# A fourth pair of rounded weight parts in the mixer of a hybrid decoder block, and the first slots of the expert ring moved to other memory

## The chip, the cores and the metric

The kernel runs on one core of a Trainium2 chip. The metric is the device time of one execution in microseconds (us), the median of several runs. The engines are called by the names of the profile: PE (TensorE matmul), PEld (its weight loads), DVE (VectorE), ACT (ScalarE), POOL (GpSimd) and SP (SyncE, whose queue SPq issues nearly all transfers).

## The reference, cut to what matters

One decoder block on 256 tokens of width 1024, all in fp32. A mixer comes first: one projection of x onto 5376 columns (`w_in`) feeds an RWKV-7 recurrence (8 heads of 64), a causal attention (8 heads of 64) and two sigmoid gates; the two branches go through their own weights, are gated, added and projected by `w_out`. Then a layer norm, a router that takes 4 of 32 experts for each token, and the experts:

```
proj   = x @ w_in                                  # 256 x 5376
merged = gate0 * (rwkv7(proj) @ w_branch_rwkv) + gate1 * (attention(proj) @ w_branch_attn)
x      = layer_norm(alpha * x + merged @ w_out)
h      = x[tokens of e] @ expert_w_in[e] + b       # 1024 x 2048, fp32, for each of 32 experts
y      = swiglu(h) @ expert_w_out[e] + b           # 1024 x 1024
out    = layer_norm(alpha * x + sum over 4 experts of weight * y)
```

The expert weights are 32 x 12 MB of fp32 and dominate the traffic.

## The kernel before, in words

**The mixer's products.** `w_in` is taken in 21 jobs of 256 columns, each in two halves of 512 KB (`load_col`, into one of RAWS = 4 buffers `wr`). A half is split into two rounded parts, a high one `wh` (a cast on ACT, line 208) and a low one `wl` (raw minus high, line 209, on POOL for the first half of a job and on DVE for the second; on DVE for both in the first two jobs). The products run on PE as three fp32r passes (high x high, high x low, low x high, `three`, line 322), 24 matmuls for a half, all recorded at line 131. The pool of parts has PARTS = 3 buffers of each kind: a half can be split only when the products of the half three before it are done. In the rows that follow, a half's buffers carry numbers, so wl_853 is the low part of one particular half.

**What the products are mixed with.** A planner written out at line 825 interleaves four generators on PE: the two halves of the recurrence (`rwkv_half`, four heads each), the attention, and the 21 jobs (`gemms`), in an order that its own estimates (WAIT, `spent`) decide while the program is built. Within each half of the recurrence stands a solve (lines 539 to 558): eight masked copies out of PSUM (L528), four scatters (L539), a transposition (L544), a loop of 15 small pairs of instructions on DVE (L551, L552), a product with a mask (L553), a transposition back (L555), and four copies on ACT (L558). PE then transposes that result (`w<-ident,ring` in the first half, `w<-ident,kr` in the second, line 564) and goes on with many small matmuls.

**Memory.** The expert weights go through a ring of 10 slots (`stream`, line 788). Slots are taken in the order 0 to 9; seven of them hold 2 MB, and slot 8 holds 3 MB. Until the mixer is over, five 2 MB blocks at the left of the memory (`slot_e(0)` to `slot_e(4)`) hold its long-lived data, two tensors each: x_t and low_t (x, and the inputs of the low-rank parts), h0a and h0b, h0c and half_t, inv_t and y_t8, and the gates. Each becomes a slot when its data are no longer wanted: block 0 is slot 0, block 1 slot 1, block 2 slot 2, blocks 3 and 4 slots 5 and 6. In `next_job` (line 368) three loads of 2 units (1 MB each) are issued between the loads of `w_in` once the low-rank parts, the first half of the recurrence and the second solve are done.

**After the mixer.** `branch_weights(n)` (line 921) loads the branch weights of four column groups, n = 0 to 3, and asks for ring loads up to 8, 8, 10 and 10 units (line 933). `out_weights(k)` (line 984), k = 0 to 7, loads 512 KB of `w_out` each, splits it into parts, and asks for up to 10, 10, 10, 12, 12, 12, 12 and 14 units. On DVE, the low part of `out_weights(0)` stands ahead of `merge(2)`, which gates and adds the third column group, and of a copy of the layer-norm vectors (`gbc`, line 967) that PE waits for before it begins the products with `w_out`. All transfers of these places go through SP's one queue, in the order in which they are issued. Then come the layer norm, the routing and 32 experts, eight 1 MB units of `expert_w_in` and four of `expert_w_out` each; a slot is loaded again when PE has used it.

Of the kernel before, what the change touches and what calls it, by code (L numbers as in the profile page):

```python
# [9 lines left out]
F32 = mybir.dt.float32  # L10
F32R = mybir.dt.float32r
# [7 lines left out]
P = 128  # L19
# [17 lines left out]
WAIT = {"d1": 36.12, "d2": 25.0, "d3": 36.78, "lo": 5.97, "kk": 4.39, "rk": 2.07, "bt": 6.5, "bk": 2.55, "unit": 0.5,  # L37
        "sub": 18, "xm": 1.3, "mg": 1.02, "mg2": 1.0, "ws": 0.71, "us": 0.49, "y": 0.73, "gn": 2.77, "rope": 2.21,
        "sm": 3.6, "tr": 0.81, "s1": 13.02}
# [11 lines left out]
PARTS = 3  # L51
UNIT = 2048
# [66 lines left out]
def hybrid_block_kernel(ctx: ExitStack, tc: tile.TileContext, A, out):  # L119
# [21 lines left out]
    def slot_e(i):  # L141
        return ring.tile([P, 2 * UNIT], F32, name="ring%d" % i)

    x_t, low_t, h0a, h0b, h0c, half_t, inv_t, y_t8, *gates = (t[:, i * UNIT:(i + 1) * UNIT] for t in map(slot_e, range(5)) for i in range(2))
    gates = [t.rearrange("p (q j t) -> p q j t", q=2, j=4) for t in gates]
    ident = const.tile([P, P], F32, name="ident")
    iota = const.tile([P, CAP], F32, name="iota")
# [10 lines left out]
    def half(name):  # L158
        return (raws_ if name == "wr" else parts).tile([P, 1024], F32, name=name)

    mx = ExitStack()
    tmp_ctx = ExitStack()
    px_ctx = ExitStack()
    pg = px_ctx.enter_context(tc.tile_pool(name="pg", bufs=2, space=PSUM))
    pw = px_ctx.enter_context(tc.tile_pool(name="pw", bufs=4, space=PSUM))
    pa = px_ctx.enter_context(tc.tile_pool(name="pa", bufs=2, space=PSUM))
    sp = tmp_ctx.enter_context(tc.tile_pool(name="sp", bufs=1, side="right"))
    ap_ = tmp_ctx.enter_context(tc.tile_pool(name="ap", bufs=1, side="right"))
    cp = tmp_ctx.enter_context(tc.tile_pool(name="cp", bufs=1, side="right"))
# [25 lines left out]
    x_t = x_t.rearrange("p (k t) -> p k t", k=KD)  # L195
# [5 lines left out]

    def split(raw, n, engine):

        hi, lo = half("wh").bitcast(F32R), half("wl").bitcast(F32R)
        s = 1024 // n
        for i in range(n):
            sl = slice(i * s, (i + 1) * s)
            nc.scalar.copy(out=hi[:, sl], in_=raw[:, sl])  # L208
            engine.tensor_tensor(out=lo[:, sl], in0=raw[:, sl], in1=hi[:, sl].bitcast(F32), op=ALU.subtract)  # L209
        return [t.rearrange("p (k c) -> p k c", k=4) for t in (hi, lo)]  # L210
# [68 lines left out]
        nc.scalar.copy(out=xh[:, sl, :], in_=x_t[:, sl, :])  # L279
        nc.vector.tensor_tensor(out=xl[:, sl, :], in0=x_t[:, sl, :], in1=xh[:, sl, :].bitcast(F32), op=ALU.subtract)  # L280

    lora_parts = [[half(n).bitcast(F32R) for n in ("wh", "wl")] for _ in range(2)]

    def split_lora(n, i):
        i, j = divmod(n * i, 4)
# [8 lines left out]
    lora_parts = [[t.rearrange("p (k c) -> p k c", k=4) for t in w] for w in lora_parts]  # L294
# [58 lines left out]
    def next_job():  # L353
        if asked:
            asked.sort(key=lambda a: a[0][0] == "a")
            key, col, use, raws, gemm = asked.pop(0)
        elif "v0" in done and len(free_gates) > (8 - EARLY_GATES if "rwkv0" not in done else LATE_GATES if min(at(n) for n in range(3)) < 1e9 else 0):
            g = free_gates.pop(0)
            key, col, use, raws, gemm = "gate%d" % g, GATE0 + g * 256, lambda ps: gate(g, ps), None, gemm_cm
        else:  # L360
            return None
        if key == "lora":
            return key, use, gemm, [lambda w=w: w for w in lora_parts]
        early_ = raws is not None
        raws = raws or load_col(col)
        if key == "v0":
            constants()
        for after, wait, n in (("low", WAIT["d1"], 2), ("rwkv0", WAIT["d2"], 4), ("sub1", WAIT["d3"], 6)):
            if done.get(after, 1e9) + wait <= spent[0] and len(tiles) < n:
                stream(n)  # L370
        engines = [nc.vector] * 2 if early_ else [nc.gpsimd, nc.vector]
        return key, use, gemm, [lambda i=i: split(raws[i], 2 if early_ else 1, engines[i]) for i in range(2)]
# [409 lines left out]
    while sum(takes) < len(views):  # L782
        n = sum(takes)
        takes.append(min(sizes[len(takes)] if len(takes) < len(slots) else 2 - n % 2, len(views) - n))
    tiles, pieces = [], []
    later = {n: lambda i=i: slot_e(i) for i, n in enumerate((0, 1, 2, 5, 6))}

    def stream(n):

        while len(tiles) < n:  # L790
            n_ = len(pieces) % len(slots)
            if slots[n_] is None:
                slots[n_] = later[n_]()
            slot = slots[n_]
            u0, m = len(tiles), takes[len(pieces)]
            pieces.append(u0)
            i = 0
            while i < m:
                src, k = views[u0 + i]
                j = i + 1  # L800
                if k is None:
                    dst = slot[:, i * UNIT:j * UNIT].rearrange("p (q k c) -> p q k c", q=len(src), k=KD // 2)
                    for q, v in enumerate(src):
                        fetch(out=dst[:, q], in_=v)
                else:
                    while j < m and views[u0 + j][0] is src and views[u0 + j][1] == k + j - i:
                        j += 1
                    fetch(out=slot[:, i * UNIT:j * UNIT], in_=src[:, k * UNIT:(k + j - i) * UNIT])
                i = j
            tiles.extend(slot[:, i * UNIT:(i + 1) * UNIT] for i in range(m))  # L810
# [10 lines left out]
    def at(n):  # L821
        r = ready[n]
        return done.get(r[0], 1e9) + r[1] if isinstance(r, tuple) else r
# [4 lines left out]
    while min(at(n) for n in range(3)) < 1e9 or "gate7" not in done:  # L828
        n = min((n for n in range(4) if at(n) <= spent[0]), default=None)
# [3 lines left out]
        if n < 3 and since >= FILL and at(3) <= spent[0]:  # L833
            n = 3
        wait = next(tasks[n], 1e9)
        since = 0 if n == 3 else since + 1
        if wait is None and min(at(i) for i in range(3)) <= spent[0]:
            wait = 0.0
        if wait is None:

            spent[0] = max(spent[0], min(at(n) for n in range(3)))
            wait = 0.0
        ready[n] = wait if isinstance(wait, tuple) else spent[0] + wait
    stream(6)
    nc.gpsimd.tensor_copy(out=tri, in_=cm[:, M_SC:M_SC + P])
    mx.close()
    tmp_ctx.close()
# [6 lines left out]
    def slot_of(i):  # L854
        return slot_pools[i].tile([P, sizes[i] * UNIT], F32, name="ring")

    later.update((i, lambda i=i: slot_of(i)) for i in (3, 4, 7, 8, 9))
    for i in (9, 3, 4):
        slot_pool(i, side="right")
    slot_b = slot_of(9)  # L860
    slot_b = [slot_b[:, i * UNIT:(i + 1) * UNIT] for i in range(2)]
# [59 lines left out]
    def branch_weights(n):  # L921

        ns = slice(n * 256, (n + 1) * 256)
        raws = load(wba[:, :, ns], wbr[:, :, ns])
        if n == 2:
            fetch(out=gbr, in_=A["norms"])
            fetch(out=bo, in_=L("expert_b_out"))
            fetch(out=rw, in_=A["router_by_rows"].rearrange("(k p) e -> p k e", p=P))
            fetch(out=rb, in_=L("router_b").partition_broadcast(P))
        if n == 0:  # L930
            for b in range(NB):
                fetch(out=x1[:, b, :], in_=A["x_by_rows"][b * P:(b + 1) * P, :])
        stream((8, 8, 10, 10)[n])
        w = []
        for i, raw in enumerate(raws):
            hi, lo = half("wh").bitcast(F32R), half("wl").bitcast(F32R)
            halved(hi, lo, raw, 1, [("pool", "dve")[(i + 1) % 2]] * 2)
            w.append([t.rearrange("p (k c) -> p k c", k=4) for t in (hi, lo)])
        branch.append(w)
# [525 lines left out]
    for kind, e in steps:  # L1465
        i = e % 2
# [147 lines left out]
```

## Time and profile before

| | us |
|---|---|
| median of 3 runs | 1241.23 |
| lowest and highest run | 1229.15, 1243.23 |
| the profiled execution's own time | 1234.5 |
| its span, first to last instruction | 1232.3 |
| mean granted clock of PE | 0.983 of 2.4 GHz |

The profile is of one execution, whose own time is 2.2 us more than its span. Times in the trace are from the span's start. The matmuls' ends are modelled and overlap the next one, so that the distance between two starts tells more than a duration.

### The profile page before, as it was taken

The numbers are of one execution on the slowest core, as the hardware profiler recorded it, in microseconds if no ns is written. First come the engines' busy times: TensorE is split into PE (matmuls) and PEld (weight loads), VectorE is DVE, ScalarE is ACT, GpSimd is POOL, SyncE is SP. The second block draws the span as 40 slices with busy tenths as digits, with TensorE's granted clock in tenths as the row PEclk, the third lists the DMA queues.
The fourth block names the chain that finished last, engine by engine and source line by source line (L and its number), as shares of the span: only waits on it lengthen the run. The fifth ranks groups of instructions, "written<-read, shape, count | busy, mean of one in ns | idle before, by whom it ended". The sixth has DMA issues, their size and how long they took to land. (4 is left out here: it accounts for less than half of the span.)

```text
span 1232.3 us, 15098 instructions
## 1 busy us (share of the span) xinstructions
PE 1145.2 (93%) x6396; PEld 580.3 (47%) x6396; DVE 404.1 (33%) x767; ACT 263.9 (21%) x486; POOL 94.2 (8%) x69
## 2 busy tenths in 40 slices
PE   9989989999999999999989887989898998989996
PEld 7778778897434343443424223423232333333423
DVE  5975783385502313130202111211112121212123
ACT  7456443554111010111101000101010101010211
POOL 3322121152300000000000000000000000000001
PEclk9989997999999999999999998999999999999999
DMA  8434244497999999999999999999999999999994
GB/s 269 121 102 155 81 160 167 147 340 266 414 429 428 426 427 429 426 427 428 427 428 427 425 430 395 390 425 429 428 426 427 428 427 428 428 427 426 429 424 162
DMA packets 62272, 439.80 MB, mean 357 GB/s; under 512 B 5662, under 2 KB 34168, under 8 KB 37528
## 3 DMA queue, kind: packets, MB, share of 16 engines
q1 hardware_dynamic: 61624, 437.67, 86.6%
q8 instruction: 52, 0.85, 0.3%
q0 software_dynamic: 144, 0.79, 0.2%
q10 hardware_dynamic: 432, 0.33, 0.1%
q14 instruction: 20, 0.16, 0.0%
HBM read 437.71 MB, written 1.05 MB: 356 GB/s over the span
## 5 line engine op out<-in xcount | busy, mean ns | idle before, releaser
L131 PE MATMUL h<-ring,xg 128*64 128x512 f32 x2048 | 459.6, 596 | 26.6 <-DMA ring<-in_expert_w_in_dram 25.4
L131 PEld LDWEIGHTS h<-ring,xg 128*64 128x64 f32 x2048 | 143.5, 136 | 308.2 <-issue 287.3
L131 PE MATMUL y<-ring,at 128*64 128x512 f32 x992 | 222.8, 596 | 27.5 <-DMA ring<-in_expert_w_out_dram 26.0
L1314 DVE TENSOR_SCALAR h<-h 128x512 f32<-128x512 f32 x32 | 22.4, 700 | 395.4 <-PE h L131 395.4
L131 PEld LDWEIGHTS y<-ring,at 128*64 128x64 f32 x992 | 68.9, 137 | 168.8 <-issue 134.4
L1315 ACT ACTIVATE lc<-h 128x512 f32<-128x512 f32 x32 | 19.1, 597 | 514.0 <-DVE h L1314 499.5
L131 PE MATMUL g<-xh,wh 128*128 128x256 f32 x304 | 95.6, 314 | 2.9 <-ACT rope_s L707 2.1
L1349 DVE TENSOR_TENSOR acc<-acc,t 128x512 f32<-128x512 f32 x56 | 38.5, 687 | 173.7 <-PE t L131 173.7
L131 PE MATMUL g<-xh,wl 128*128 128x256 f32 x304 | 87.9, 289 | 1.4 <-DVE wl L209 1.4
L131 PE MATMUL g<-xl,wh 128*128 128x256 f32 x304 | 87.5, 288 | 0.0
L1338 ACT COPY yp<-y 64x512 f32<-64x512 f32 x62 | 35.9, 579 | 212.3 <-PE y L131 211.7
L131 POOL TENSOR_TENSOR acc<-acc,x 128x256 f32<-128x256 f32 x4 | 3.9, 993 | 903.2 <-DVE ln_rs L131 903.0
L131 PEld LDWEIGHTS g<-xh,wh 128*128 128x128 f32 x304 | 59.4, 195 | 12.6 <-issue 8.1
L1115 PE MATMUL t<-oh,x 128*128 128x128 f32 x480 | 59.5, 284 | 5.9 <-DVE oh L1101 5.9
L1115 PEld LDWEIGHTS t<-oh,x 128*128 128x128 f32 x480 | 56.6, 197 | 17.7 <-issue 17.3
L131 PEld LDWEIGHTS g<-xl,wh 128*128 128x128 f32 x304 | 59.6, 196 | 2.2 <-issue 2.2
L131 PEld LDWEIGHTS g<-xh,wl 128*128 128x128 f32 x304 | 59.6, 196 | 1.9 <-DVE wl L209 1.6
L131 PE MATMUL t<-yp,ct 128*128 128x512 f32 (+1 forms) x124 | 56.5, 598 | 0.7 <-ACT yp L1338 0.7
L209 POOL TENSOR_TENSOR wl<-wr,wh 128x1024 fp32r<-128x1024 f32 x18 | 43.2, 2402 | 138.3 <-ACT wh L208 128.9
L208 ACT CAST wh<-wr 128x1024 fp32r<-128x1024 f32 (+1 forms) x44 | 42.1, 969 | 44.6 <-PE g L131 32.7
L131 PEld LDWEIGHTS t<-yp,ct 128*128 128x128 f32 x124 | 22.3, 189 | 34.6 <-issue 32.3
L1118 ACT ACTIVATE xg<-t,gbc 128x128 f32<-128x128 f32 x60 | 27.4, 457 | 42.5 <-PE t L1115 24.9
(373 smaller groups left out, 1070.0 us busy)
## 6 DMA issues: line engine op xcount, KB each, us to landing
ring<-in_expert_w_in_dram SPq DMA_DIRECT2D x127, 2048.0 KB, 39.1
ring<-in_expert_w_out_dram SPq DMA_DIRECT2D x61, 2048.0 KB, 39.1
wr<-in_w_in_dram SPq DMA_DIRECT2D x40, 512.0 KB, 4.0
wr<-in_w_out_by_rows_dram SPq DMA_DIRECT2D x8, 512.0 KB, 5.1
ring<-in_expert_w_out_dram SPq DMA_DIRECT2D x4, 1024.0 KB, 26.1
wr<-in_w_branch_attn_dram SPq DMA_DIRECT2D x4, 512.0 KB, 7.3
wr<-in_w_branch_rwkv_dram SPq DMA_DIRECT2D x4, 512.0 KB, 8.8
ring<-in_expert_w_in_dram SPq DMA_DIRECT2D x2, 1024.0 KB, 16.1
```

The costliest lines, as they stand in the source:

```text
L131: queues[e] = make(*a, **k)
L208: nc.scalar.copy(out=hi[:, sl], in_=raw[:, sl])
L209: engine.tensor_tensor(out=lo[:, sl], in0=raw[:, sl], in1=hi[:, sl].bitcast(F32), op=ALU.subtract)
L1115: last = nc.tensor.matmul(ps[:, i * ns:(i + 1) * ns], lhsT=x1[:, b, k * P:(k + 1) * P], rhs=oh[:, b, :], start=b == 0 and i == 0, stop=b = ...
L1118: def scaled(ps, n, k0, put=lambda e, make, **a: make(**a)):
L1314: nc.vector.tensor_scalar(out=gate_, in0=gate_, scalar1=7.0, scalar2=None, op0=ALU.min)
L1315: nc.scalar.activation(out=lc4, in_=g4, func=AF.Sigmoid, scale=1.702)
L1338: nc.scalar.copy(out=yp[r0_:r0_ + CAP, dh * 512:(dh + 1) * 512], in_=y[dh * CAP:(dh + 1) * CAP, :])
L1349: nc.vector.tensor_tensor(out=acc[:, b, hs], in0=acc[:, b, hs], in1=ps, op=ALU.add)
```

## The change

x_t and low_t leave block 0 of the ring and get a pool of their own (`ep`) at the right end of the memory, with the pools that are given back when the mixer is over. Once x has been split, the memory of x_t is used as a fourth pair of parts: `pair_of` gives every fourth half the two halves of that tile in place of `wh` and `wl`. The blocks of the ring are four instead of five: h0a and h0b are slot 0, h0c and half_t slot 1, the last two blocks slots 5 and 6 as before. Slots 2, 3 and 4 lie in the memory given back with the mixer, slot 4 in that of `ep`. The load after the low-rank parts is dropped, and the targets of `stream` after the mixer are 2 units lower until n = 3.

```
-    x_t, low_t, h0a, h0b, h0c, half_t, inv_t, y_t8, *gates = (... map(slot_e, range(5)) for i in range(2))
+    h0a, h0b, h0c, half_t, inv_t, y_t8, *gates = (... map(slot_e, range(1, 5)) for i in range(2))
+    given = [0]
+    def pair_of():
+        given[0] += 1
+        if given[0] % (PARTS + 1) or not more:
+            return half("wh").bitcast(F32R), half("wl").bitcast(F32R)
+        t = more[0].tile([P, UNIT], F32, name="xt").bitcast(F32R)
+        return t[:, 0:1024], t[:, 1024:2048]
+    ep = tmp_ctx.enter_context(tc.tile_pool(name="ep", bufs=1, side="right"))
+    more = [ep]
+    x_t, low_t = (ep.tile([P, UNIT], F32, name=n) for n in ("xt", "low"))
     def split(raw, n, engine):
-        hi, lo = half("wh").bitcast(F32R), half("wl").bitcast(F32R)
+        hi, lo = pair_of()
-        for after, wait, n in (("low", WAIT["d1"], 2), ("rwkv0", WAIT["d2"], 4), ("sub1", WAIT["d3"], 6)):
+        for after, wait, n in (("rwkv0", WAIT["d2"], 2), ("sub1", WAIT["d3"], 4)):
-    later = {n: lambda i=i: slot_e(i) for i, n in enumerate((0, 1, 2, 5, 6))}
+    later = {n: lambda i=i: slot_e(i) for i, n in ((1, 0), (2, 1), (3, 5), (4, 6))}
-    stream(6)
+    stream(4)
+    more.clear()
-    later.update((i, lambda i=i: slot_of(i)) for i in (3, 4, 7, 8, 9))
-    for i in (9, 3, 4):
+    later.update((i, lambda i=i: slot_of(i)) for i in (2, 3, 4, 7, 8, 9))
+    for i in (4, 9, 2, 3):
         slot_pool(i, side="right")
-        stream((8, 8, 10, 10)[n])
+        stream((6, 6, 8, 10)[n])
```

PE's instructions stand in the same order as before from the first to the last. On ACT, DVE and POOL the splits move forward against the rest. On DVE, the first solve before (the small pairs are L551 and L552, the splits L209; the rows are taken from its start, its middle and its end):

```order
L209 TENSOR_TENSOR wl_783<-wr_776,wh_782 128x1024
L551 TENSOR_TENSOR ring3_64<-ring3_64 128x15
...
L715 TENSOR_TENSOR ak_810<-ak_810,rope_t_811 128x512
L552 TENSOR_TENSOR ring3_64<-ring3_64 128x6x10
L209 TENSOR_TENSOR wl_853<-wr_846,wh_852 128x1024
L551 TENSOR_TENSOR ring3_64<-ring3_64 128x5x11
...
L553 TENSOR_TENSOR ring2_63<-ring3_64,cf_107 128x512
L555 STREAM_TRANSPOSE ring3_64<-ring2_63 128x512
L209 TENSOR_TENSOR wl_948<-wr_941,wh_947 128x1024
```

Here wl_783 stands ahead of the loop's first pair, wl_853 ahead of the pair that is 55 wide on its way down, and wl_948 behind the transposition L555. The same place in the changed kernel, whose lines are 13 higher (the fourth pair is xt, here xt_783 and xt_947, and the small pairs are L564 and L565):

```order
L222 TENSOR_TENSOR xt_783<-wr_777,xt_783 128x1024
L552 TENSOR_TENSOR ring3_63<-sc_t_151,cf_111 32x16x16 x4
...
L564 TENSOR_TENSOR ring3_63<-ring3_63 128x11x5
L222 TENSOR_TENSOR wl_853<-wr_846,wh_852 128x1024
L565 TENSOR_TENSOR ring3_63<-ring3_63 128x11x5
...
L566 TENSOR_TENSOR ring2_62<-ring3_63,cf_111 128x512
L222 TENSOR_TENSOR xt_947<-wr_941,xt_947 128x1024
L568 STREAM_TRANSPOSE ring3_63<-ring2_62 128x512
```

The half 783 is split ahead of the four scatters instead of behind them, the half 853 six steps of the loop sooner, and the half 947 ahead of the transposition back instead of behind it. On SP, the loads of the first ring slots between those of `w_in`, as a difference:

```order
-L131 DMA wr<-in_w_in_dram 128x4x256 x18
-L131 DMA ring_1493<-in_expert_w_in_dram 128x4096
+L131 DMA wr<-in_w_in_dram 128x4x256 x26
+L131 DMA ring_1858<-in_expert_w_in_dram 128x4096
 L131 DMA wr<-in_w_in_dram 128x4x256 x8
-L131 DMA ring_1864<-in_expert_w_in_dram 128x4096
-L131 DMA wr<-in_w_in_dram 128x4x256 x8
-L131 DMA ring_2457<-in_expert_w_in_dram 128x4096
+L131 DMA ring_2449<-in_expert_w_in_dram 128x4096
```

The first of the three ring loads is gone; the other two stand where they stood. Further on SP, behind the branch weights of n = 3, also as a difference:

```order
 L131 DMA wr<-in_w_branch_attn_dram 128x4x256
 L131 DMA wr<-in_w_branch_rwkv_dram 128x4x256
+L131 DMA ring<-in_expert_w_in_dram 128x4096
 L131 DMA wr<-in_w_out_by_rows_dram 128x1024 x4
-L131 DMA ring_2907<-in_expert_w_in_dram 128x4096
+L131 DMA ring_2905<-in_expert_w_in_dram 128x4096
```

There a 2 MB load is new, between the last branch weights and the first weights of `w_out`; from the load after those four on, both kernels have asked for equally many units.

## Rows read from the trace of the kernel before

**Rows 1.** The page's second part: what the transfers moved, in GB/s, in 40 equal slices of the span, 30.8 us each.

```profile
GB/s 269 121 102 155 81 160 167 147 340 266 414 429 428 426 427 429 426 427 428 427 428 427 425 430 395 390 425 429 428 426 427 428 427 428 428 427 426 429 424 162
```

**Rows 2.** The page's sixth part, transfers by their issue: out<-in, queue, operation, count, size of one, median us from issue to landing.

```profile
ring<-in_expert_w_in_dram SPq DMA_DIRECT2D x127, 2048.0 KB, 39.1
```

**Rows 3.** The timeline of SP at the end of the mixer and behind it: start of the issue, us, queue, line, operation, count (the us of a row with a count reach from the first issue to the last).

```profile
247.91 0.50 SPq L131 DMA_DIRECT2D ring<-in_expert_w_in_dram  x1
...
251.03 0.38 SPq L131 DMA_DIRECT2D wr<-in_w_branch_rwkv_dram  x1
255.03 8.83 SPq L131 DMA_DIRECT2D wr<-in_w_out_by_rows_dram  x4
...
294.01 1.28 SPq L131 DMA_DIRECT2D ring<-in_expert_w_out_dram  x3
```

**Rows 4.** What PE waited for in the first 250 us: engine, tile and line that waited, engine, tile and line that released it; us in total, times, longest us.

```profile
PE g L131 <- DVE wl L209: 8.3, 3, 3.4
PE g L131 <- ACT rope_s L707: 2.1, 1, 2.1
```

**Rows 5.** The timeline of PE: start, us, engine, line, operation, and in brackets how long the engine sat idle before it and for whom. The rows at 96.82 and 104.62 are the first and last of one and the same run of products in the first half of the recurrence as 193.68 and 206.82 are in the second.

```profile
21.01 2.59 PE L131 MATMUL w<-ring 64*128 64x256 f32 x12
...
76.85 0.39 PE L131 MATMUL g<-wl,xh 128*128 128x256 f32 x1 [3.44 <-DVE wl L209]
...
77.63 4.22 PE L131 MATMUL w<-ring 64*128 64x256 f32 x12
...
86.69 1.04 PE L131 MATMUL w<-ident,ring 128*128 128x128 f32 x8
...
96.82 0.55 PE L131 MATMUL a<-ident,sm 128*128 128x128 f32 x3
...
104.62 0.27 PE L131 MATMUL w<-ring,sc_t 64*64 64x64 f32 x1
...
167.76 0.39 PE L131 MATMUL g<-xh,wl 128*128 128x256 f32 x1 [1.42 <-DVE wl L209]
...
177.06 0.55 PE L131 MATMUL g<-wl,xh 128*128 128x256 f32 x1 [3.43 <-DVE wl L209]
...
183.56 1.03 PE L131 MATMUL w<-ident,kr 128*128 128x128 f32 x8
...
193.68 0.55 PE L131 MATMUL a<-ident,sm 128*128 128x128 f32 x3
...
206.82 1.59 PE L131 MATMUL w<-va,sc_t 64*64 64x64 f32 x16
```

**Rows 6.** Stretches of 2 us: us, then length, busy us of PE, PEld, DVE, ACT and POOL with the count of instructions, the granted clock of PE, the share of DMA, GB/s.

```profile
84.00:86.00 2.00, 2.00 (x15) 2.00 (x15) 1.86 (x6) 2.00 (x5) 0.00 (x0) 0.76 0.36 126
180.00:182.00 2.00, 2.00 (x16) 2.00 (x16) 0.00 (x0) 1.96 (x4) 0.00 (x0) 0.86 0.88 302
198.00:200.00 2.00, 2.00 (x9) 1.67 (x8) 0.00 (x0) 0.19 (x1) 0.77 (x1) 0.50 0.13 13
```

**Rows 7.** The timelines of DVE, ACT and POOL in the order of time, columns as in Rows 5: a split early in the mixer, the first solve, and the second solve.

```profile
29.77 1.23 DVE L209 TENSOR_TENSOR wl<-wr,wh 128x1024 fp32r<-128x1024 f32 x1 [2.57 <-ACT wh L208]
...
59.76 3.05 DVE L539 TENSOR_TENSOR ring<-sc_t,cf 32x256 f32<-32x256 f32 x4
...
75.58 1.22 DVE L209 TENSOR_TENSOR wl<-wr,wh 128x1024 fp32r<-128x1024 f32 x1
...
79.76 0.71 DVE L555 STREAM_TRANSPOSE ring<-ring 128x512 f32<-128x512 f32 x1
...
80.39 1.18 DVE L209 TENSOR_TENSOR wl<-wr,wh 128x1024 fp32r<-128x1024 f32 x1
80.50 2.58 ACT L558 COPY ring<-ring 32x256 f32<-32x256 f32 x4 [6.07 <-DVE ring L555]
...
157.23 4.70 DVE L539 TENSOR_TENSOR ring<-sc_t,cf 32x256 f32<-32x256 f32 x4
157.76 2.40 POOL L209 TENSOR_TENSOR wl<-wr,wh 128x1024 fp32r<-128x1024 f32 x1 [0.91 <-ACT wh L208]
...
179.49 2.63 ACT L558 COPY kr<-ring 32x256 f32<-32x256 f32 x4 [7.39 <-DVE ring L555]
```

**Rows 8.** Transfers by their issue, columns as in Rows 2: the first row of those issued from 248 to 250 us, the second from 250 to 254, the third from 254 to 257.

```profile
ring<-in_expert_w_in_dram SPq DMA_DIRECT2D x1, 2048.0 KB, 9.0
...
wr<-in_w_branch_rwkv_dram SPq DMA_DIRECT2D x1, 512.0 KB, 8.8
...
wr<-in_w_out_by_rows_dram SPq DMA_DIRECT2D x1, 512.0 KB, 6.1
```

**Rows 9.** The timeline of ACT, DVE and PE from the first split of `w_out` to PE's first product with the layer-norm vectors, columns as in Rows 5.

```profile
261.22 1.14 ACT L131 CAST wh<-wr 128x512 fp32r<-128x512 f32 x2 [0.24 <-DMA wr<-in_w_out_by_rows_dram]
...
261.87 2.18 DVE L131 TENSOR_TENSOR wl<-wr,wh 128x512 fp32r<-128x512 f32 x1 [0.62 <-ACT wh L131]
...
267.54 0.69 DVE L131 TENSOR_TENSOR wl<-wr,wh 128x512 fp32r<-128x512 f32 x1
267.59 0.67 PE L131 MATMUL w<-gbc,rw 128*32 128x2 f32 x16 [0.65 <-DVE gbc L131]
```

**Rows 10.** Stretches of 10 us, columns as in Rows 6.

```profile
280.00:290.00 10.00, 10.00 (x56) 8.38 (x55) 6.55 (x13) 4.46 (x9) 3.00 (x2) 1.00 0.71 280
290.00:300.00 10.00, 8.76 (x60) 7.50 (x60) 6.48 (x26) 3.96 (x7) 1.44 (x3) 1.00 0.52 180
```

More of the change, by code (lines that the diff above doesn't have):

```diff
@@ L142, in slot_e @@
         return ring.tile([P, 2 * UNIT], F32, name="ring%d" % i)
-    x_t, low_t, h0a, h0b, h0c, half_t, inv_t, y_t8, *gates = (t[:, i * UNIT:(i + 1) * UNIT] for t in map(slot_e, range(5)) for i in range(2))
+    h0a, h0b, h0c, half_t, inv_t, y_t8, *gates = (t[:, i * UNIT:(i + 1) * UNIT] for t in map(slot_e, range(1, 5)) for i in range(2))
     gates = [t.rearrange("p (q j t) -> p q j t", q=2, j=4) for t in gates]
@@ L280, in split_x @@
         nc.vector.tensor_tensor(out=xl[:, sl, :], in0=x_t[:, sl, :], in1=xh[:, sl, :].bitcast(F32), op=ALU.subtract)
-    lora_parts = [[half(n).bitcast(F32R) for n in ("wh", "wl")] for _ in range(2)]
+    lora_parts = [pair_of() for _ in range(2)]
     def split_lora(n, i):
```

## The prediction

> **What bounds the kernel now.** I read the slices of the page first. From the eleventh slice on, about 308 us, the transfers move 414 to 430 GB/s in nearly every slice up to the last but one [rows 1]; a 2 MB load of expert weights takes 39.1 us from issue to landing with eight in flight, which is 4.9 us for each 2 MB [rows 2]. So the experts' part is bound by its transfers. The change leaves them in the same order with the same bytes, and its time is taken as it is. What the change can move is the lead-in: the moment at which the mixer and the projection behind it are over and the stream runs full. I take the issue at 294.01 us for that moment, since SP's expert_w_out loads there wait for memory that is free only behind the last products with `w_out` [rows 3]. Each microsecond by which that moment moves counts as one microsecond of the end.
>
> Second comes what PE waits for in the lead-in, because its instructions stand in one fixed order, the same in both kernels. It waits little: 8.3 us in three waits for a low part `wl` split on DVE, and 2.1 us once for a bank [rows 4]. Each of the two long waits is followed by products at half the clock: twelve products that take 2.59 us at 21.01 take 4.22 at 77.63, right behind the wait of 3.44 us [rows 5], and the granted clock is back at full inside the stretches at 84 to 86 and at 180 to 182 us (0.76 and 0.86 on their mean) [rows 6]. With 4.22/2.59 = 1.63, the stretch from 77.6 to about 85 lost 7.4 - 7.4/1.63 = 2.9 us, and that from 177.1 to about 180.6 lost 1.4.
>
> Third comes the other end of the lead-in, the first weights of `w_out`, below.
>
> **Term A, the first solve.** The half 853 was split at 75.58, behind most of the solve's loop on DVE [rows 7]; in the new order it stands six steps of the loop sooner, ahead of the moment at which PE asks for it (76.85 - 3.44 = 73.4). The wait of 3.44 goes, and the 2.9 us at half clock with it: PE would come to the transposes `w<-ident,ring`, now at 86.69 [rows 5], at 86.69 - 3.44 - 2.9 = 80.35. But they need the four copies on ACT, which end at 80.50 + 2.58 = 83.08 [rows 7]. That is what is late next. These copies hang on the transposition at 79.76, and in the new order the split of the half 947, 1.18 us [rows 7], stands ahead of it and no longer behind: 83.08 + 1.2 = 84.3. How much a split on POOL lengthens the solve I bound by the four scatters on DVE: 3.05 us in the first solve, and 4.70 in the second, where a split on POOL ran from 157.76 [rows 7]. Since the splits on POOL move as well, I allow 1.65 us both ways: the transposes start between 82.6 and 85.9, that is 4.1 to 0.8 us sooner than now, middle 2.4. PE then stands idle for 84.3 - 80.35 = 3.9 us, about as long as in the two waits above, and I charge what the clock cost behind them, 1.4 to 2.9, middle 2.1. A = -2.4 + 2.1 = -0.3, from -4.1 (no clock loss) to +2.1.
>
> A rule bears on the 1.65. The Trainium skill (SBUF — State Buffer, "Who interferes with whom") says that an operation of DVE that needs the pair of ports which it shares with GpSimd excludes GpSimd's, and the other way round. By it a split on POOL could hold DVE for its whole 2.40 us [rows 7] rather than 1.65, and A would reach from -4.8 to +2.9; the rows show 1.65.
>
> **Term B, the second solve.** The same splits gain there too: the waits of 1.42 at 167.76 and 3.43 at 177.06 [rows 5] and the 1.4 us of clock behind the second. PE would be at the transposes `w<-ident,kr` at 183.56 - 6.25 = 177.3, but the copies for them end at 179.49 + 2.63 = 182.12 [rows 7], only 1.44 before PE comes now. The chain ends 1.65 sooner if the split on POOL no longer hits its scatters, and 1.2 later if a split comes ahead of its transposition as in the first solve: a start between 180.5 and 183.3, middle 181.9, which is 1.7 sooner. PE idles 4.6 us instead, again with 2.1 for the clock. B = +0.4, from -3.1 to +2.6.
>
> **Term C, the bank.** The wait of 2.1 us named for ACT [rows 4] is for a bank that DVE also has to read out, late in a full queue. One split of 1.23 us as at 29.77 [rows 7] stands sooner there and leaves that queue. C = -1.2, from -2.1 to 0.
>
> **Term D, the weights of `w_out`.** The load dropped in the mixer comes back as a 2 MB load behind the branch weights of n = 3, ahead of the first load of `w_out`. SP's loads land in the order of their issue: the 2 MB issued at 247.91 land after 9.0 us, at 256.9; the branch weights issued at 251.03 after 8.8, at 259.8; the first `w_out` load, issued at 255.03, after 6.1, at 261.1 [rows 3, 8]. That last landing is waited for: the cast of its data starts at 261.22 after an idle 0.24 us, DVE's low part follows at 261.87, and behind that in DVE's queue stand `merge(2)` and the copy `gbc`, for which PE waits 0.65 us before 267.59 [rows 9]. So there is no slack from the landing to PE. A 2 MB load more is 4.9 us. Some comes back: the low part at 261.87 took 2.18 us beside a busy POOL, and the same form took 0.69 at 267.54 [rows 9], so a later one would be 1.5 us shorter. To the 3.4 us I add 2.1 for the clock behind a PE wait of some 4 us. D = +5.5, from 0 (the loads do not queue) to 4.9 + 2.9 = 7.8. The bytes themselves are not late: from 280 to 300 us the transfers move 280 and 180 GB/s of the 428 that they can [rows 10], room for 10 us x (148 + 248) GB/s = 4.0 MB.
>
> What costs nothing: the other end of the memory for x and low_t, the smaller targets until n = 3 (those slots are read only in the experts' part, after 300 us), and the early load's absence between loads of `w_in` (PE had no wait for one of those).
>
> **The sum.** -0.3 + 0.4 - 1.2 + 5.5 = +4.4 us, bounds -9.3 and +12.5. Against the profiled execution: 1234.5 + 4.4 = 1238.9. That execution lies 6.7 below the median of the three runs, 1241.23, which themselves lie 14 apart; the mean of all four is 1237.0, and with 4.4 it is 1241.4. I predict 1240. About 2% of the time, 25 us, is what a measurement of this kernel can tell from no change.
>
> **Rivals.**
> 1. *The waits go and nothing is late in their place.* The solves' chains come out at their short ends, the clock stays up, and the `w_out` loads find room: -4.1 - 3.1 - 2.1 = -9.3, so 1237 - 9.3 = 1228. For it: 8.3 of the 10.4 us of PE's waits are for just these splits [rows 4]. Against it: the ACT copies leave only 3.6 and 1.44 us.
> 2. *The extra load does not hold up `w_out`.* Loads on one queue may overtake each other, so that the 512 KB lands at its old time: D = 0, sum -1.1, 1236. Against it stand the landings at 256.9, 259.8 and 261.1 in order of issue. The Trainium skill (DMA: Bandwidth & Descriptors, "Queues, rings and completion order") says that descriptors are consumed in ring order while completion is not first in, first out for an issuing engine; the first half is what the landings show, and by the second half this rival would hold, but no row here shows an overtaking.
> 3. *Slower: PE's clock stays down.* Behind the new wait at the transposes comes the sparse part of the recurrence. The same products take 104.62 - 96.82 = 7.8 us in the first half, and 206.82 - 193.68 = 13.1 in the second, where the granted clock is 0.50 [rows 5, 6], 1.68 times as long. If the wait at about 81 brought that clock on, and it stayed down for what now takes 37 us, up to about 120 us, that adds 37 x 0.68 = 25 us: 1262. From there on it decides. Against it: the waits of 3.4 us were followed by 4 to 7 us of half clock, not by 60.
>
> **Chances.** Forecast 0.58, rival 1 0.20, rival 2 0.17, rival 3 0.05. The range of 8 in 10 is the forecast's bounds, -9.3 to +12.5 around 1237, widened by a little for the spread of the runs: 1226 to 1254. Faster by over 2% lies beyond even rival 1, 0.02; slower by over 2% is rival 3 with a part of its chance, 0.04; within 2%, 0.94.
>
> **What would show it.** Right: no wait of PE for a split's `wl` of over 1 us, in its place waits of 3 to 5 us at `w<-ident` for ACT's copies, the clock at half behind them; the first `w_out` cast some 4 us later against the branch products, and PE's wait for `gbc` at 4 us instead of 0.65; the issue now at 294.01 at 297 to 299. A cast of `w_out` that waits for no DMA would make D wrong, transposes that start without a wait would make A and B wrong, and a change of the end that the shift at 294 does not show would make the first paragraph wrong.

## The result, and the profile after

| | before | changed |
|---|---|---|
| median of the runs, us | 1241.06 (4 runs, 1229.15 to 1243.23) | 1258.05 (4 runs, 1250.79 to 1260.05) |
| ratio, 95% interval | | 1.0145, 1.0096 to 1.0194 |
| profiled execution's own time, span, us | 1234.5, 1232.3 | 1260.05, 1258.2 |
| mean granted clock of PE in it | 0.983 | 0.961 |

Slower by 17 us, outside the range. Ratios leave out three slow runs of the experiments (two of `after2`, one of `after_end`), each over 1.5% above the fastest run of the same kernel. The two profiled executions lie further apart than the medians, 25.55 us: the kernel before's is 6.6 us under its median, and the changed kernel's is the longest of its four. What follows divides the difference of their two spans, 25.9 us, and not the 17. The whole of it lies ahead of the experts, as the first paragraph of the prediction has it: the issue at 294.01 of [rows 3] stands at 319.74 now, 25.7 us later, and the span is 25.9 longer. The slices of the page, answering to [rows 1], are back at 426 to 429 GB/s from the twelfth on, but for one (358, where the kernel before has 395 and 390) and the last:

```profile
PEclk9887896798899999999999998999999999999998
...
GB/s 280 118 101 60 59 184 186 2 315 322 299 429 427 427 428 427 428 427 426 428 428 426 428 427 426 358 427 428 427 426 428 426 428 427 427 429 426 427 426 168
```

The first row is the granted clock in tenths: 7 in the fourth slice, 6 and 7 in the seventh and eighth; full speed is 2.4 GHz. The kernel before had, in the same row of its page:

```profile
PEclk9989997999999999999999998999999999999999
```

What PE waited for in the first 340 us of the changed kernel (columns as in [rows 4]):

```profile
PE w L131 <- DVE gbc L131: 4.6, 1, 4.6
PE g L131 <- DVE ring L407: 4.0, 1, 4.0
PE w L131 <- ACT ring L571: 3.4, 1, 3.4
PE w L131 <- ACT kr L571: 3.2, 1, 3.2
PE a L131 <- DVE sm L752: 1.7, 1, 1.7
```

The three long waits for `wl` are gone (one of 0.7 us is left, at 37.47), the two at the transposes are there as forecast, and so is the one for `gbc`. The bank's wait has not shrunk from 2.1 us but grown to 4.0. The timeline of PE, answering to [rows 5]:

```profile
44.34 0.58 PE L131 MATMUL g<-xh,wh 128*128 128x256 f32 x1 [4.03 <-DVE ring L407]
...
76.11 0.28 PE L131 MATMUL g<-wl,xh 128*128 128x256 f32 x1
...
76.80 2.59 PE L131 MATMUL w<-low 64*128 64x256 f32 x12
...
86.39 0.66 PE L131 MATMUL w<-ident,ring 128*128 128x128 f32 x4 [3.44 <-ACT ring L571]
...
104.49 0.90 PE L131 MATMUL a<-ident,sm 128*128 128x128 f32 x3
...
113.85 1.14 PE L131 MATMUL w<-ring,sc_t 64*64 64x64 f32 x16
...
143.93 0.70 PE L131 MATMUL a<-ident,sm 128*128 128x128 f32 x3 [1.71 <-DVE sm L752]
...
193.60 1.97 PE L131 MATMUL w<-ident,kr 128*128 128x128 f32 x8 [3.24 <-ACT kr L571]
```

The twelve products behind the former wait take 2.59 us again, not 4.22. The transposes start 0.3 us sooner than before. But the products that began at 96.82 begin at 104.49: 8 us are lost in a stretch that has no new wait of a microsecond. Stretches of 8 and 10 us of the changed kernel (columns as in [rows 6], the clock third from the end):

```profile
80.00:88.00 8.00, 4.36 (x34) 3.91 (x34) 4.22 (x11) 4.14 (x9) 3.74 (x3) 0.98 0.33 90
88.00:98.00 10.00, 9.83 (x59) 8.59 (x58) 6.10 (x12) 7.16 (x16) 2.45 (x1) 0.50 0.23 70
98.00:108.00 10.00, 10.00 (x96) 9.45 (x97) 2.10 (x7) 1.42 (x5) 0.00 (x0) 0.50 0.24 69
130.00:140.00 10.00, 10.00 (x51) 8.56 (x49) 6.36 (x10) 2.43 (x7) 0.97 (x2) 0.66 0.01 2
240.00:250.00 10.00, 10.00 (x46) 6.70 (x44) 1.23 (x1) 2.73 (x7) 0.00 (x0) 0.50 0.00 0
```

and the kernel before where the same products stand that take from 88 to 108 us here:

```profile
90.00:100.00 10.00, 10.00 (x160) 9.46 (x158) 4.44 (x8) 4.54 (x11) 2.38 (x1) 1.00 0.54 165
```

PE was granted 1.2 GHz instead of 2.4 from 88 to 108, behind its wait at the transposes and through what stands there, over 100 small products of 16 or 32 columns and some 30 of 256 between them. At 108 it rose again, among small products. Since PE's order is the same in both kernels, the start of one product can be set against its start before, all along:

| place (time before) | shift, us | what the step cost |
|---|---|---|
| 43.6, behind the bank | +2.7 | C: +1.9 of wait, and half clock behind it |
| 76.85, the former wait for wl | -0.7 | that wait gone |
| 86.69, transposes | -0.3 | A without its clock |
| 97.9, in the small products | +8.6 | A's clock: 8.9 |
| 129.9, end of the first half | +14.0 | half clock from 132 to 139, the wait of 1.7 |
| 178.9 | +7.4 | the waits of [rows 5] at 167.76 and 177.06 gone |
| 186.6, behind the second transposes | +12.7 | B: a wait of 3.2, half clock from 193 to 200 |
| 235.6, end of the second half | +18.9 | half clock from 238 to 255 instead of 225 to 228 |
| 267.59, gbc | +23.7 | D's wait: 4.8 |
| 270.1 | +25.6 | D's clock: 2.0 |

For D, the timeline of ACT, DVE and PE answers to [rows 9]:

```profile
286.34 1.14 ACT L131 CAST wh<-wr 128x512 fp32r<-128x512 f32 x2 [5.18 <-DMA wr<-in_w_out_by_rows_dram]
286.99 0.69 DVE L131 TENSOR_TENSOR wl<-wr,wh 128x512 fp32r<-128x512 f32 x1 [6.00 <-ACT wh L131]
...
291.26 1.01 PE L131 MATMUL w<-gbc,rw 128*32 128x2 f32 x16 [4.59 <-DVE gbc L131]
```

The cast waited 5.18 us for its load instead of 0.24, the low part took 0.69 instead of 2.18, and PE waited 4.59 instead of 0.65.

### The profile page after: what moved, and what is told of

Its sections match the earlier page's. It is cut to its first block, busy times and chain, and to the rows that moved or that the text cites. A ratio compares the mean times of both kernels' runs of the same rounds, so it can differ in the third digit from the quotient of the medians.

```text
span 1258.2 us, 15088 instructions
## 1 busy us (share of the span) xinstructions
PE 1167.0 (93%) x6396; PEld 598.9 (48%) x6396; DVE 405.5 (32%) x767; ACT 264.1 (21%) x486; POOL 96.6 (8%) x69
## 5 line engine op out<-in xcount | busy, mean ns | idle before, releaser
L131 PE MATMUL g<-xh,wh 128*128 128x256 f32 x224 | 72.2, 322 | 4.7 <-DVE ring L407 4.0
L131 PE MATMUL g<-xh,wl 128*128 128x256 f32 x224 | 66.5, 297 | 0.9 <-DVE wl L222 0.7
L131 PE MATMUL g<-xl,wh 128*128 128x256 f32 x224 | 66.2, 295 | 0.0
L131 PEld LDWEIGHTS g<-xh,wh 128*128 128x128 f32 x224 | 45.5, 203 | 11.4 <-issue 5.3
L131 PEld LDWEIGHTS g<-xl,wh 128*128 128x128 f32 x224 | 45.8, 204 | 1.7 <-issue 1.7
L131 PEld LDWEIGHTS g<-xh,wl 128*128 128x128 f32 x224 | 45.7, 204 | 1.5 <-DVE wl L222 0.9
L131 PE MATMUL g<-xh,xt 128*128 128x256 f32 x160 | 39.8, 326 | 0.0
```

Of the source, the lines that this page charges most:

```text
L131: queues[e] = make(*a, **k)
```

## The experiments

All ratios are to the kernel before, measured beside each, with a 95% interval. My theory after the result: the fourth pair trades PE's waits among large products for waits ahead of small ones, where the clock then stays down; the ring's change adds D. The rival: the small products, or the memory's new place, bring the clock down by themselves.

The first half of that rival holds in one place of the kernel before itself. In its second half of the recurrence it runs the same small products from 186.98 to 193.98 us, and PE is idle nowhere between its wait at 177.06 [rows 5] and 208 us; its clock falls at 194 all the same (columns as in [rows 6]):

```profile
183.00:194.00 11.00, 11.00 (x143) 10.12 (x141) 5.64 (x13) 5.15 (x12) 2.39 (x1) 1.00 0.67 212
194.00:207.00 13.00, 13.00 (x119) 11.22 (x117) 2.37 (x11) 4.36 (x11) 2.34 (x1) 0.51 0.39 146
```

In its first half they run at the full clock, as the row from 90 to 100 above shows. So small products can bring the clock down without a wait, and the experiments can only show what a wait ahead of them adds.

**The ring's change alone (`ring_only`).** `more = []` in the place of `more = [ep]`: no fourth pair.

> The changed kernel without its fourth pair of parts (every half goes to wh and wl); memory and ring loads as changed. Theory: the mixer's loss of some 19 us comes from the fourth pair, by PE's new waits at the transposes and the half clock behind them, so the mixer runs as in the kernel before, PE waits for wl again at 77 and 177 us, and only the extra 2 MB load ahead of w_out remains: 1241 + 7 = 1248. Rival: the memory's new place or the missing early load slows the mixer: 1258, with the half clock from 88 to 108 as in the changed kernel.

Measured: 1244.77 us, 1.0065 (1.0028 to 1.0102). PE's waits are back as before, with `gbc` beside them:

```profile
PE g L131 <- DVE wl L222: 8.8, 3, 3.7
PE w L131 <- DVE gbc L131: 5.2, 1, 5.2
```

The size is the theory's, some 8 us, and not the rival's. But the mixer isn't as before in this profile, of the second longest of the ten runs. It has two more stretches at half clock: from 92 to 102 us, behind a wait of only 0.75 us at 89.36 (the shift grows by 5.3 there), and from 228 to 245, with no wait ahead of it since the one at 180.85 (6.0). The load ahead of `w_out` costs 6.6 in it.

**The load of slot 4 later (`late_load`, `ring_late`, `ring_end`, `after_end`).** In the first two it stands behind four loads of `w_out`; in the last two slots 5 and 6 stand behind all eight as well. `late_load` and `after_end` are the changed kernel, the `ring_` ones have no fourth pair.

```
-        stream((6, 6, 8, 10)[n])
+        stream((6, 6, 8, 8)[n])
-        stream((10, 10, 10, 12, 12, 12, 12, 14)[k])
+        stream((8, 8, 8, 12, 12, 12, 12, 14)[k])     # late_load, ring_late
+        stream((8, 8, 8, 10, 10, 10, 10, 14)[k])     # ring_end, after_end
```

> The changed kernel with the load of slot 4 behind the first four loads of w_out instead of ahead of them. Theory: PE's wait for gbc of 4.6 us and the 2 us of half clock behind it go, 6.7 us in all: 1258 - 6.7 = 1251, mixer unchanged. Rival: the lead-in's end is set elsewhere and the load's bytes are late anyway: 1258.

Measured: 1256.33 us, 1.0140 (1.0078 to 1.0203); the expected gain of 0.5% doesn't show, though the interval would hold it. PE's wait for `gbc` went from 4.6 to 1.1 us, but two ring loads in a row now stand ahead of the last four of `w_out`, PE waits there, and the shift grows by 5.0 us:

```profile
302.15 0.50 PE L131 MATMUL w<-wh,mh 128*128 128x512 f32 x1 [0.53 <-ACT wh L131]
302.88 0.50 PE L131 MATMUL w<-wl,mh 128*128 128x512 f32 x1 [0.23 <-DVE wl L131]
304.65 0.50 PE L131 MATMUL w<-wl,mh 128*128 128x512 f32 x1 [0.80 <-DVE wl L131]
306.34 0.51 PE L131 MATMUL w<-ring,mh 128*128 128x512 f32 x1 [0.73 <-DVE ring L131]
```

> The changed kernel without the fourth pair (every half goes to wh and wl) and with the load of slot 4 behind the first four loads of w_out. Theory: what the change of the memory alone costs is the place of that load, so this one is level with the kernel before, within 2 us. Rival: the memory's new place or the missing early load costs time by itself: some 5 us over the kernel before, as without the load's move.

Measured: 1242.37 us, 1.0031 (0.9994 to 1.0068), which tells neither expectation from the other.

> The changed kernel without the fourth pair, with the load of slot 4 behind four loads of w_out and those of slots 5 and 6 behind all eight. Theory: then no ring load stands ahead of a w_out load that PE waits for, and the transfers have room from 280 us on: level with the kernel before, within 2 us. Rival: the ring's bytes are late at the beginning of the experts instead: 3 to 5 us over.

Measured: 1237.26 us, 1.0007 (0.9972 to 1.0042): level. PE's wait for `gbc` is 0.67 us. So the memory's new place and the missing early load cost nothing that this can tell (0.4% at most). The place of the ring loads costs the difference to `ring_only`, 0.6%, some 7 us, though the two intervals overlap a little. The traces are plainer: from the products that the kernel before begins at 261 us to those at 275, the shift grows by 6.6 us in the changed kernel and in `ring_only`, and by 0.0 in `ring_end`. That is term D, shown. `ring_end` moves the load of slot 5 too; with slot 4's alone moved, `ring_late` still loses 4.1 us from there to 290.

> The changed kernel with the load of slot 4 behind four loads of w_out and those of slots 5 and 6 behind all eight. Theory: the wait of 4.6 us for gbc and the clock behind it go, nothing else: 6 us less than the changed kernel, about 1252. Rival: as with the load moved by four places only, the time hardly moves: 1256.

Measured: 1248.90 us, 1.0141 (1.0045 to 1.0237), too wide to tell from either expectation. The wait for `gbc` is 1.1 us, and D is 1.2 us in the profile instead of 6.6; the half clock from 86 to 107 us is there again.

**The changed kernel again (`after2`).**

> The changed kernel itself once more, beside the others of this call. Expected 15 to 19 us over the kernel before. If the half clock of 88 to 108 us is a chance of the one profile, this profile has it elsewhere; if it belongs to the order of the work, it is here again.

Measured: four runs from 1246.83 to 1267.49 us; 1.0166 (1.0050 to 1.0282) by two of them. The half clock behind the first transposes is in this profile too (86 to 100 and 103 to 117 us), and in `late_load` (88 to 109) and `after_end` (86 to 107), whose order is the changed kernel's up to there. From the transposes to the products that the kernel before begins at 107 us, the shift grows by 9.5 us in the changed kernel's first profile and by 11.7, 9.4 and 9.3 in these three. In the five in which PE doesn't wait at the transposes (`ring_only`, `ring_late`, `ring_end`, and the two with the fourth pair in part, below) it grows by 0.0 to 5.3. So most of it belongs to the changed order of the work, and not to one execution.

**PE's wait at the transposes, put into the kernel before (`late_copies`, `late_copies2`).**

```
-        for i in range(4):                                  # the four copies on ACT, L558
+        for i in [0, 1, 2, 3] * (1 if hf else 4):           # late_copies2: 2
```

> The kernel before with ACT's four copies of the first solve made four times over (12 copies more, about 7.7 us), nothing else. They end at about 90.8 us where PE comes to the transposes at 86.7. Theory: a wait of 4 us there is followed by the half clock through the small products behind it: 4 + 9 = 13 us over the kernel before. Rival: the wait costs itself and 2 us of clock as the forecast had it: 6 us over the kernel before.

Measured: 1250.37 us, 1.0133 (1.0057 to 1.0208). PE's wait and the clock behind it:

```profile
89.54 0.66 PE L131 MATMUL w<-ident,ring 128*128 128x128 f32 x4 [4.23 <-ACT ring L558]
```

```profile
90.00:100.00 10.00, 9.43 (x57) 8.07 (x56) 4.10 (x15) 6.52 (x18) 0.00 (x0) 0.50 0.00 0
100.00:110.00 10.00, 10.00 (x84) 9.67 (x84) 2.54 (x5) 2.88 (x5) 2.36 (x1) 0.50 0.19 54
110.00:120.00 10.00, 10.00 (x103) 8.44 (x102) 2.60 (x10) 4.33 (x11) 2.35 (x1) 0.50 0.68 264
120.00:130.00 10.00, 10.00 (x66) 8.87 (x65) 2.76 (x8) 3.82 (x8) 0.00 (x0) 0.62 0.19 52
```

The transposes start 2.9 us later than before, and at 107 us of the kernel before the shift is 19.0: behind a wait that delays PE by 3 us, 16 us more are lost with the clock at half. Of these, 5.8 come back where the kernel before is at half clock itself, from 194 to 208. The forecast's price of 2 us is refuted at this place.

> The kernel before with ACT's four copies of the first solve made twice over (4 copies more, 2.6 us), nothing else. They end at about 85.7, ahead of PE at 86.7. Theory: without a wait of PE there the clock keeps up, and the time is the kernel before's within 2 us. Rival: ACT's later queue, not PE's wait, is what cost the 16 us with four times the copies: then some 4 us over, and the half clock is there again behind 88 us.

Measured: 1246.77 us, 1.0066 (1.0024 to 1.0109): neither. The copies ended at 85.75 and PE waited 0.5 us for them, but the later ones on ACT were late, and PE waited behind the transposes:

```profile
91.97 3.22 PE L131 MATMUL w<-ring,sc_t 64*64 64x32 f32 x32 [1.82 <-ACT ring L565]
```

There the half clock follows in the profile (92 to 99 and 102 to 116 us), with a shift of 10.4 us by 105. The ten runs fall into two groups, five from 1239.5 to 1243.9 and five from 1249.7 to 1252.3, with mean granted clocks of 0.976 to 0.979 and 0.968 to 0.972. So some executions stay at half clock for longer than others. Whether this wait decides it was not seen: one run alone was profiled, of the upper group.

**The wait taken from the changed kernel (`short_solve`, `fill_wait`, `fill_two`, `fill_two_end`).** `short_solve` leaves out ten of the fifteen pairs of steps of the first solve (`for j in range(SUB - 1 if hf else 5)`). The others give PE products without use:

```
             ps = work()                          # the transposes' bank
+            for _ in range(16 if c == 0 else 0):
+                queued("pe", nc.tensor.matmul, ps, lhsT=xh[:, 0, 0:P], rhs=xh[:, 0:2, :]..., start=True, stop=True)
...
             pz = work()                          # the first small products behind: fill_two, fill_two_end
+            for _ in range(14 if h == 0 else 0):
+                queued("pe", nc.tensor.matmul, pz, ...)
```

> The changed kernel whose first solve runs 5 of its 15 pairs of steps (the rest of that solve is left out), so that the solve and ACT's copies end some 5 us sooner. Theory: PE's wait of 3.4 us at the first transposes goes, and with it the half clock from 88 to 108 us that cost 9 us: some 12 us less than the changed kernel in the same call. Rival: the small products behind the transposes bring the clock down without a wait: only the 3.4 us come back, the half clock stays.

Measured: 1248.20 us, 1.0111 (1.0040 to 1.0182). Not decisive: the wait at the transposes went, a wait of 2.03 us stood at 89.52 for ACT's next copy instead, and the clock was at half from 89 to 96 and from 100 to 113.

> The changed kernel with 16 products of 512 columns without use on PE ahead of each half's transposes, about 3.7 us, into the bank that the transposes then overwrite: PE is busy where it waited 3.4 and 3.2 us for ACT's copies. Theory: the waits bring the half clock; with PE busy the clock is 1.0 from 87 to 108 us and the 9.0 us lost there come back, and some 2.7 behind the second: 1258 - 11.7 = 1246. Rival: the small products behind the transposes bring the clock down by themselves: half clock from 88 to 108 as before, 1258.

Measured: 1252.58 us, 1.0126 (1.0072 to 1.0180). Here too the wait moved on, to 3.23 us at 93.47, and the clock was full until 95 and at half from there to 108. The lateness is ACT's, and PE meets it at the next place.

> The changed kernel with products without use (512 columns, into banks that are overwritten right behind) at two places of each half: 16 ahead of the transposes, as before, and 14 ahead of the first small products behind them, where PE waited 3.2 us with the first place alone. The work is as late as in the changed kernel, only PE is busy while it waits. Theory: the clock falls because of the waits, so it is at full through the small products from about 93 to 108 us, and the shift there is 3 to 4 us instead of 8.6: 5 us or more less than the changed kernel, 1251 or less. Rival: the small products bring the clock down whatever stands ahead of them: half clock again from 95 to 108, and the time of the changed kernel.

Measured: 1254.25 us, 1.0144 (1.0075 to 1.0214). With both waits filled the clock stays up through the small products:

```profile
82.33 3.83 PE L131 MATMUL w<-xh 128*128 128x512 f32 x16
86.10 0.66 PE L131 MATMUL w<-ident,ring 128*128 128x128 f32 x4
...
89.94 3.38 PE L131 MATMUL w<-xh 128*128 128x512 f32 x14
```

```profile
90.00:100.00 10.00, 9.70 (x113) 8.48 (x113) 3.42 (x11) 6.33 (x15) 2.34 (x1) 1.00 0.19 54
100.00:110.00 10.00, 10.00 (x137) 8.89 (x135) 4.13 (x13) 4.44 (x12) 0.00 (x0) 0.83 0.19 54
```

The shift in the small products is 3.2 to 5.0 us there instead of 8.6 in the changed kernel, at the same lateness of the work. Of the two readings the theory's holds at this place: what PE does ahead of the small products decides, for most of them, the clock in them. The Trainium skill (TensorE: Matmul & The Clock Gate, "Part 1: The HAM clock gate (the 'warmup' mystery)") says that the lower clock is the default and that activity releases it; the granted clock of 1.00 here against 0.50 in the changed kernel agrees. In the whole time it does not show: in this profile another stretch, from 128 to 145 us, takes 8 us back, and D is still there.

> Both edits on the changed kernel: the products without use at the two places, and the ring loads behind those of w_out. Theory: the two gains add, 11 us or more less than the changed kernel: 1246. Rival: the clock falls elsewhere instead: 1252 or more.

Measured: 1245.83 us, 1.0064 (1.0026 to 1.0102), against 1.0141 for `after_end`, the same kernel without the filling. The intervals overlap (1.0045 to 1.0102), so a gain of some 9 us is possible and not shown.

**Where the fourth pair is used (`pair_early`, `pair_late_end`).** It is given out up to the 14th half only, or from the 21st on only (`... or given[0] > 14 ...`, `... or given[0] < 21 ...` in `pair_of`); `pair_late_end` has the ring loads of `ring_end`.

> The changed kernel with the fourth pair given out only up to the 14th half, that is until the first solve; memory and ring loads as changed. Theory: it is here that the fourth pair loses: its splits come sooner, POOL's beside DVE's, the bank is read later (PE's wait of 4.0 us at about 44), the solve starts some 3 us later, PE waits at the first transposes and the clock stays at half behind them: 8 us or more over the run without the fourth pair, some 1253. Rival: the loss belongs to the splits inside the first solve and behind it: level with the run without the fourth pair, 1245.

Measured: 1247.37 us, 1.0104 (1.0043 to 1.0165). The time tells neither expectation from the other. Its profile shows the bank's wait of 4.0 us, 3.6 of shift right behind it (2.7 by 77 us), and D's wait, but no wait at the transposes and half clock from 99 to 102 only: the early splits alone don't bring A.

> The changed kernel with the fourth pair given out only from the 21st half on, that is behind the first solve, and the load of slot 4 behind four loads of w_out, those of slots 5 and 6 behind all eight. Theory: the first solve runs as in the kernel before, the waits of 1.4 and 3.4 us for wl at the second solve go, and a wait of 2 to 3 us at its transposes stands in their place: within 3 us of the run with the same loads and no fourth pair, 1235 to 1241. Rival: the fourth pair loses wherever it is used: 1246 or more.

Measured: 1247.11 us, 1.0115 (1.0054 to 1.0177), where the same without the fourth pair is level: the rival's size. The waits for `wl` at the second solve are gone and PE waits 3.2 us at its transposes, as expected. The profile is of the shortest of the four runs (1238.11 us), and in it the price behind that wait is small: the shift is -0.3 ahead of these transposes and 3.3 at 208 us. What makes the other three runs longer was not seen.

**More products ahead of the transposes (`sub22`).** `"sub": 22` for 18 in the planner's table; this changes PE's order.

> The changed kernel with the planner's estimate of a solve (WAIT sub) at 22 instead of 18, so that more products stand on PE ahead of the transposes. Theory: the waits of 3.4 and 3.2 us at the transposes and the half clock behind them shrink: 1248. Rival: the products that are spent ahead are missing among the small ones behind, where the clock then falls all the same: 1256 to 1262.

Measured: 1261.25 us, 1.0217 (1.0165 to 1.0268), above the changed kernel's 1.0145, though the intervals overlap. Both long waits at the transposes went, and others came:

```profile
PE a L131 <- DVE sm L752: 13.4, 2, 9.1
PE w L131 <- ACT va L578: 5.5, 1, 5.5
```

No version is faster than the kernel before; `ring_end` comes level with it.

## Why the prediction was wrong, point by point

**The frame was right.** The experts' part took the same time, and the shift at the end of the lead-in, 25.7 us, is the shift of the end, 25.9. The forecast's sign for it, an issue at 297 to 299 us, failed with the sum: it came at 319.74.

**Term D was right in mechanism and near in size:** 6.7 us in the profile (4.8 of wait and 2.0 of clock) where the forecast had 5.5 (3.4 and 2.1), some 7 us by `ring_only` against `ring_end`. The rival without a delay of `w_out` falls.

**Term B was right within its bounds:** from a shift of 14.0 to one of 12.7, so -1.3 against +0.4, with a clock loss of 2.7 against 2.1.

**Term A failed at "I charge what the clock cost behind them, 1.4 to 2.9, middle 2.1".** It measured 8.9, and 9.3 to 11.7 over the four profiles of that order. The two rows from which I took the price are waits with large products of 256 columns behind them; behind the transposes stand, between such products, over 100 of 16 or 32 columns. The kernel's own trace showed a longer stretch at half clock in such products [rows 5, 6]. I used that only for the rival in which the clock stays down, gave it 0.05 and priced it at 25 us. What came lies between: half clock for 20 us. `late_copies` shows that a wait there is followed by as much with nothing changed but ACT's copies, and `fill_two` that the clock stays up in the same products when PE is kept busy ahead of them. Its start was off as well, -0.3 against -2.4, since the solve begins later:

```profile
63.65 4.52 DVE L552 TENSOR_TENSOR ring<-sc_t,cf 32x256 f32<-32x256 f32 x4
...
81.92 1.22 DVE L222 TENSOR_TENSOR xt<-wr,xt 128x1024 fp32r<-128x1024 f32 x1
83.06 0.70 DVE L568 STREAM_TRANSPOSE ring<-ring 128x512 f32<-128x512 f32 x1
```

The scatters stood at 59.76 before [rows 7] and took 3.05 there; the transposition comes 3.3 us later, with the split ahead of it that the order shows.

**Term C had the wrong sign.** The splits that come sooner bring POOL's sooner too; beside two of them (30.84 to 36.33) DVE's split at 33.99 took 3.42 us, where the one at 35.31 before took 1.21, and the bank was read later: +1.9 of wait where I had -1.2. I had priced POOL's splits beside DVE for the solves and not for this place. The two rows of the changed kernel, and the one before:

```profile
30.84 5.49 POOL L222 TENSOR_TENSOR wl<-wr,wh 128x1024 fp32r<-128x1024 f32 x2 [3.52 <-ACT wh L221]
33.99 3.42 DVE L222 TENSOR_TENSOR wl<-wr,wh 128x1024 fp32r<-128x1024 f32 x1
```

```profile
35.31 1.21 DVE L209 TENSOR_TENSOR wl<-wr,wh 128x1024 fp32r<-128x1024 f32 x1
```

**What was not in the sum:** the half clock from 132 to 139 us with the wait of 1.7 behind it, 5.4 us of shift, and the half clock from 238 to 255, 6.2, in the last small products of each half. The first follows a stretch that is late by A. The second has no wait ahead of it, and it isn't the fourth pair's: `ring_only` and `ring_late`, which have none, are at half clock through the same products,

```profile
228.00:238.00 10.00, 10.00 (x46) 7.66 (x45) 1.26 (x2) 2.64 (x7) 0.00 (x0) 0.52 0.00 0
```

```profile
226.00:236.00 10.00, 10.00 (x47) 7.36 (x47) 1.23 (x1) 2.44 (x6) 0.00 (x0) 0.50 0.00 0
```

and `after_end`, which has it, is not. In every profile but those of `fill_wait` and `sub22` this stretch costs either 6.0 us or nothing against the kernel before. So some 6 of the 25.9 us look like a matter of the one execution that was profiled, which is part of why the spans lie further apart than the medians. Since PE's order is fixed, I had taken everything behind the transposes as unchanged.

**What stays open:** `ring_only` shows half clock in the small products behind a wait of 0.75 us only, and the kernel before has it in its second half behind none. So a wait of 3 to 4 us makes the half clock likely there but isn't its only cause. How the 10 us or so that the fourth pair costs over the ring's 7 divide among A, C and the later stretches was not shown run by run: each edit that removed one of them let another in.

## What to carry to other kernels

Price a wait of TensorE by the work that follows it: the same 3 to 4 us cost 1.4 to 2.9 us of clock ahead of large products and 9 to 16 ahead of a long run of small ones at the first transposes (at the second, 2.7 in the changed kernel's profile). So don't count a wait ahead of large products as equal to one ahead of small. A buffer more lets work on the helper engines start sooner, and on engines with a chain to finish sooner is not better: follow what it now stands in front of. A load that is postponed takes its place in a queue: put it behind the loads that are waited for, not ahead of them.

## What the runs showed of the hardware that was not expected

The spread of one kernel's times goes with the clock. Over 57 runs of the kernel before, from 1228.5 to 1246.8 us, the time falls by 10.7 us for each 0.01 of mean granted clock (0.971 to 0.989), with a correlation of -0.93. The changed kernel's four runs have 0.961 to 0.971: the 0.016 by which their mean lies below 0.981, the mean of the 57, is 17 us by that slope, and 17 us is what the change cost. This is an estimate: it extends the line past the lowest clock of the 57, and PE's waits differ between the two kernels as well.
